# Queries of six heads by block products, and half of the sums of weight blocks on GpSimd

## The chip, the cores and the metric

The kernel runs on one core of one Trainium2 chip. The metric is the device time of one execution in microseconds (us), as the median over runs. Engines go by the profile's names: PE is TensorE's matmuls and PEld its weight loads, DVE is VectorE, ACT ScalarE, POOL GpSimd, SP SyncE (it issues the DMAs).

## The reference

A small decoder: 16 meta tokens ahead of 512 tokens, D = 1024, two layers. Each layer normalizes, projects into q, k, v and a gate z, mixes the tokens, normalizes each head's output, multiplies by silu(z) and projects back. Layer 1 is gated linear attention with 4 heads (keys of 256, values of 512), layer 2 differential attention with 8 heads of 256 columns:

```python
proj = xn @ w_in                      # layer 2: [528, 1024] x [1024, 8192]
q, k, v, z = jnp.split(proj, 4, axis=-1)
s = einsum('bhpqd,bhpkd->bhpqk', qb, kh) * scale + bias   # scale = 128 ** -0.5
p = softmax(where(dist >= 0, s, -inf))
a = p[:, :, 0] - lam * p[:, :, 1]     # two softmaxes per head
o = head_rms(einsum('bhqk,bhkv->bhqv', a, vh)) * gnorm * (1.0 - lambda_init)
y = (silu(z) * o) @ w_out
```

Nearly all of the arithmetic lies in the projections with w_in and w_out.

## The kernel before, in words

Every matrix is kept as a sum of a high and a low part in the matmul's fp32r format, and a product is made of three matmul passes (high by high, high by low, low by high). `split` (L235) makes the parts: ACT copies the high one (L240), DVE subtracts it for the low one (L241; with a scale, ACT L243 and DVE L244).

A projection of 256 output columns is made in one of two ways. The **plain** way (`project`, L340; its matmul is L347) runs, for each half of 128 columns, 24 matmuls of up to 512 tokens: 8 blocks of the inner dimension by three passes, 48 in all for the 512 real tokens. The other is a **unit** (`Unit`, L360): it takes the [1024, 256] weight block as 2 x 2 blocks of [512, 128], and the tokens as 2 x 2 blocks as well, and makes the four output blocks from seven block products in place of eight. Each product (`product`, L351; its matmul is L357) has 12 matmuls of 256 columns (real tokens, the operand set Xr) or 264 (all 528 tokens, the set X). The price is sums of blocks: of the tokens once, of the weights in every unit, of the products on the way out of PSUM (ACT's copies `u` at L378, DVE's adds L403, L405 and L407).

The weights of a unit come in `want_unit` (L285). Two DMAs bring the four blocks into a tile `raw` of [128, 4, 512] (two such tiles in the ring). From it are made, in this order, the parts a11, sums, s21, a12, s43, a22. Three of them are splits of a single block (tiles a11h and a11l, and so on). `sums` makes three adds on [128, 512] on DVE (L296): raw2 + raw3 into `sum`, that plus raw0 into `sum`, and raw2 + raw0 in place. `s21` is the split of the pair `sum` into `wh` and `wl` of [128, 1024]. `s43` first makes the fourth add, raw1 + sum0 in place, also on DVE at L296, and then splits the pair raw1, raw2. A part is made as soon as the `Weights` object finds room for it: two pairs, one sum, one each of a11, a12 and a22; the room of `sum` is given back with the fourth add.

In layer 1 the jobs q, k, v and z have 20 units; in layer 2, the z, v and k of heads 1 to 7 are 21 units, and q of all eight heads is plain. That is 41 units. `q_diff_q` (L1441) makes q of one head in layer 2 and splits it with the scale into the tiles s.q.

The order of the work is that of the program on TensorE: the class `Weaver` (L73) holds a queue of generators (the projections) and puts pieces of them between the steps of the heads' attention, so many microseconds of estimated cost at a time (`fill`); `finish` runs one to its end. Each job is queued with a cost (10.3 for a plain q, 8.9 for a unit on Xr). A unit that has a unit behind it in the queue (`following`) runs the latter's first product inside its own end. The other engines' orders are set by a scheduler from the program's order and its priorities (functions marked `urgent` come 100 ahead).

POOL has little to do. `rstd_of` (L465) makes 1/sqrt of a sum of squares: a DVE scale (L467), then a `pow` on POOL (L468). In layer 1 the rows of each head's output go through ACT's sum of squares (L1087), `rstd_of`, ACT's scaling (L1089), transposes on TensorE (L1111) and DVE's product with the gate (L1113). In layer 2, `values` does the same with a pow at L1509 between ACT's L1507 and L1510, and TensorE's transposes are L1516; scores, values and turns are L326, L1502, L1486 and L1487.

Of the kernel before, what the change touches and what calls it, by code (L numbers as in the profile page):

```python
# [12 lines left out]
F32R = mybir.dt.float32r  # L13
I32 = mybir.dt.int32
AF = mybir.ActivationFunctionType
ALU = mybir.AluOpType
# [3 lines left out]
P = 128  # L20
# [3 lines left out]
NR = 512  # L24
# [48 lines left out]
class Weaver:  # L73
# [5 lines left out]
    def add(self, gen, us=0.0):  # L79
        self.queue.append(gen)  # L80
        self.left += us
        return gen
# [102 lines left out]
def trunk(ctx, tc, x, meta, g_norm, gla_w_in, gla_w_gate_up, gla_b_gate, gla_gnorm, gla_w_out,  # L185
# [3 lines left out]
    act, dve, pe, pool, sp = nc.scalar, nc.vector, nc.tensor, nc.gpsimd, nc.sync  # L189
# [17 lines left out]
    def T(p, shape, dt, tag, **kw):  # L207
        uid[0] += 1
        return p.tile(shape, dt, tag=tag, name=f"{tag}_{uid[0]}", **kw)
# [19 lines left out]
    def urgent(fn):  # L229

        def run(*a, **kw):
            with tc.high_priority(offset=100):
                return fn(*a, **kw)
        return run
# [47 lines left out]
    def block_pair(src):  # L282
        wh, wl = w_pair([P, 2, 512])
        split(wh, wl, src)
        return [[t[:, i, :] for t in (wh, wl)] for i in range(2)]  # L285

    def want_unit(w, c0):
        def single(tag, b):
            def fn(raw):
                t = [T(wp, [P, 512], F32R, tag + part, bufs=1) for part in "hl"]  # L290
                split(*t, raw[:, b, :])
                return t
            return Part(tag, fn)

        def add(o, a, b):
            dve.tensor_tensor(o, a, b, op=ALU.add)  # L296

        def sums(raw):
            t = T(wp, [P, 2, 512], F32, "sum", bufs=1)
            add(t[:, 1, :], raw[:, 2, :], raw[:, 3, :])  # L300
            add(t[:, 0, :], t[:, 1, :], raw[:, 0, :])
            add(raw[:, 2, :], raw[:, 2, :], raw[:, 0, :])
            return t

        def outer(raw):
            add(raw[:, 1, :], raw[:, 1, :], su.t[:, 0, :])
            ws.room["sum"] += 1
            return block_pair(raw[:, 1:3, :])

        a11, a12, a22 = single("a11", 0), single("a12", 1), single("a22", 3)  # L310
        su = Part("sum", sums)
        s21 = Part("pair", lambda raw: block_pair(su.t))
        s43 = Part("pair", outer)
        ws.want((w, c0), [a11, su, s21, a12, s43, a22])
        return a11, a12, a22, s21, s43

# [1051 lines left out]
    def tok_tile():  # L1368
        return T(ep, [P, 2 * (256 + NM)], F32, "t", bufs=3)
# [68 lines left out]
                tail(i)  # L1438
        return W.add(gen(), 10.3)

    def q_diff_q(hd, s):  # L1441
        want_diff(256 * hd)

        def gen():
            for i in range(2):
                bank = pb_tile("bx" if hd else ("bv", "by")[i])
                yield from project(ws.take(), real2, None, NR, [by_halves(bank)])
                assert not hd or heads[hd - 1].scored
                if i == 0:
                    s.q = [T(ep, [P, 2, NR], F32R, f"q{j}", bufs=1) for j in range(2)]  # L1450
                urgent(split)(*[t[:, i, :] for t in s.q], bank, scale=-float(P) ** -0.5)
        return W.add(gen(), 10.3)

    def diff_steps(hd, s, ys):
# [167 lines left out]
    for hd in range(D_HEADS):  # L1622
# [9 lines left out]
        if not last:  # L1632
            n = heads[hd + 1]
            late = hd == D_HEADS - 2
            if not late:
                gates.append(q_diff_z(hd + 1, n))
                values.append(q_diff_v(hd + 1, n))
            W.stop = q_diff_k(hd + 1, n)
            projs.append(q_diff_q(hd + 1, n))
            if late:  # L1640
                values.append(q_diff_v(hd + 1, n))
                gates.append(q_diff_z(hd + 1, n))
# [94 lines left out]
```

## Time and profile before

| | |
|---|---|
| median of 3 runs | 1001.82 us (1000.56 to 1002.53) |
| the profiled execution | 1001.37 us |
| its span, from the first to the last instruction | 999.6 us (1.77 us lie around it) |
| matmuls | 7143 |
| instructions of DVE, ACT, POOL | 1586, 1304, 68 |
| HBM read | 83.64 MB |

The profile is of one execution. Busy times are sums of instruction durations; an engine's busy time can hide under another's. A row of groups reads: line, engine, operation, out<-in, shapes, count | busy us, mean ns of one | idle time ahead of them and what ended it. A row of the timeline begins with start and length in us. `PE ps L1111 <- ACT t L1089` in the waits is TensorE at L1111 that waited for ACT's tile t from L1089: total us, times, longest.

### The profile page before, as it was taken

What the parts mean: (1) busy time and instruction counts of PE and PEld (TensorE: products, weight loads), DVE (VectorE), ACT (ScalarE), POOL (GpSimd) and SP (SyncE); (2) the same over time, 40 slices, a digit from 0 to 9 for tenths busy, and PEclk for the clock granted to TensorE, in tenths of its full rate; (3) what the DMA queues carried; (4) which work ended last, traced back from release to release, by engine and by line L of the source; (5) the groups of instructions that cost most, each with busy time, mean ns of one, the idle gap of its engine ahead of it and who ended that gap; (6) DMA issues with size and microseconds to landing.
All of it is one profiled execution on the core that took longest, in us unless ns stands there. A gap on an engine that the chain in (4) does not pass through costs nothing.

```text
span 999.6 us, 18267 instructions
## 1 busy us (share of the span) xinstructions
PE 981.0 (98%) x7143; PEld 920.2 (92%) x7143; DVE 784.1 (78%) x1586; ACT 597.5 (60%) x1304; POOL 46.6 (5%) x68
## 2 busy tenths in 40 slices
PE   8999999999999999999999999999999999999997
PEld 6998999999999989999899898899998999988896
DVE  7998886777777787556998886888966879777785
ACT  7775755265535656536567666466664666645583
POOL 1000000001000100000000100000010010000001
PEclk9999999999999999999999999999999999999998
DMA  7322322141233322222231322333222332323212
GB/s 194 82 69 64 86 85 86 48 113 52 85 85 85 85 54 74 86 85 79 84 104 49 94 82 95 85 96 85 85 96 72 87 91 70 109 64 92 85 65 84
DMA packets 121161, 84.24 MB, mean 84 GB/s; under 512 B 6365, under 2 KB 110077, under 8 KB 121072
## 3 DMA queue, kind: packets, MB, share of 16 engines
q1 hardware_dynamic: 121072, 83.05, 28.8%
q8 instruction: 56, 0.92, 0.4%
q14 instruction: 33, 0.27, 0.1%
HBM read 83.64 MB, written 2.12 MB: 86 GB/s over the span
## 4 chain that ended last, share of the span: by engine, by line
PE 78%; DVE 6%; ACT 3%; DMA 3%; issue 1%; POOL 1%; SPq 0%; POOLq 0%; DVEq 0%; ACTq 0%
PE bx L357 15%; PE bx L347 10%; PE bv L357 9%; PE by L357 8%; PE ps L326 7%; PE bx L830 4%; PE bx L326 3%; PE bv L830 2%; PE by L830 2%; DMA raw<-in_gla_w_in_dram 2%; PE ps L1048 2%; PE by L326 2%; PE bv L326 2%; DVE wl L241 1%; PE by L347 1%
## 5 line engine op out<-in xcount | busy, mean ns | idle before, releaser
L240 ACT ACTIVATE wh<-raw 128x1024 fp32r<-128x1024 f32 x99 | 104.4, 1055 | 61.6 <-PE by L830 26.8
L241 DVE TENSOR_TENSOR wl<-raw,wh 128x1024 fp32r<-128x1024 f32 x99 | 121.0, 1222 | 22.0 <-ACT wh L240 14.6
L357 PE MATMUL bv<-x,wh 128*128 128x264 f32 (+1 forms) x656 | 97.5, 286 | 0.0
L357 PE MATMUL bx<-x,wh 128*128 128x264 f32 (+1 forms) x640 | 95.6, 286 | 1.2 <-ACT u L378 1.2
L357 PEld LDWEIGHTS bx<-x,wh 128*128 128x128 f32 x640 | 84.8, 188 | 2.3 <-ACT u L378 1.4
L357 PEld LDWEIGHTS bv<-x,wh 128*128 128x128 f32 x656 | 86.4, 189 | 0.3
L241 DVE TENSOR_TENSOR wl<-sum,wh 128x1024 fp32r<-128x1024 f32 x41 | 50.1, 1222 | 21.0 <-ACT wh L240 17.6
L378 ACT ACTIVATE u<-bx 128x264 f32<-128x264 f32 (+1 forms) x120 | 45.5, 380 | 33.1 <-PE bx L357 29.2
L347 PE MATMUL bx<-x,wh 128*128 128x512 f32 (+1 forms) x256 | 62.4, 385 | 0.0
L1473 ACT ACTIVATE p<-p,st 128x528 f32<-128x528 f32 (+3 forms) x64 | 36.4, 569 | 40.0 <-DVE st L1471 39.9
L357 PE MATMUL bv<-x,wl 128*128 128x264 f32 (+1 forms) x328 | 56.4, 286 | 0.0
L240 ACT ACTIVATE wh<-sum 128x1024 fp32r<-128x1024 f32 x41 | 43.2, 1055 | 19.2 <-PE by L830 9.6
L357 PE MATMUL bx<-x,wl 128*128 128x264 f32 (+1 forms) x320 | 54.5, 285 | 0.0
L347 PEld LDWEIGHTS bx<-x,wh 128*128 128x128 f32 x256 | 44.5, 188 | 7.9
L1509 POOL TENSOR_TENSOR st<-st,mhalf 128x1 f32<-128x1 f32 x32 | 26.5, 828 | 474.9 <-ACT on L1507 426.9
L357 PE MATMUL by<-x,a12h 128*128 128x264 f32 (+1 forms) x320 | 46.9, 285 | 0.0
L357 PEld LDWEIGHTS bv<-x,wl 128*128 128x128 f32 x328 | 46.2, 189 | 0.0
L357 PE MATMUL bx<-x,a11h 128*128 128x264 f32 (+1 forms) x320 | 46.2, 285 | 0.0
L357 PEld LDWEIGHTS bx<-x,wl 128*128 128x128 f32 x320 | 45.3, 188 | 0.1
L240 ACT ACTIVATE a11h<-raw 128x512 fp32r<-128x512 f32 x41 | 25.7, 628 | 32.6 <-DMA raw<-in_diff_w_in_dram 18.2
L357 PEld LDWEIGHTS bx<-x,a11h 128*128 128x128 f32 x320 | 42.2, 189 | 0.8
L357 PEld LDWEIGHTS by<-x,a12h 128*128 128x128 f32 x320 | 41.9, 188 | 0.2 <-issue 0.2
(465 smaller groups left out, 2643.4 us busy)
## 6 DMA issues: line engine op xcount, KB each, us to landing
raw<-in_gla_w_in_dram SPq DMA_DIRECT2D x48, 512.0 KB, 5.3
raw<-in_diff_w_in_dram SPq DMA_DIRECT2D x42, 512.0 KB, 4.2
raw<-in_diff_w_in_dram SPq DMA_DIRECT2D x11, 1024.0 KB, 5.7
raw<-in_gla_w_out_dram SPq DMA_DIRECT2D x8, 1024.0 KB
raw<-in_diff_w_out_dram SPq DMA_DIRECT2D x8, 1024.0 KB, 4.9
T<-bdr SPq DMA_DIRECT2D x8, 264.0 KB
out_dram<-x SPq DMA_DIRECT2D x8, 256.0 KB, 2.0
kd<-steep SPq DMA_DIRECT2D x4, 400.0 KB
```

The costliest lines, as they stand in the source:

```text
L240: act.activation(hi, src, AF.Copy)
L241: dve.tensor_tensor(lo, src, hi.bitcast(F32), op=ALU.subtract)
L326: pe.matmul(ps, l, r, start=first and n == 0, stop=last and n == 2, **kw)
L347: pe.matmul(bank, a[:, k, :], b[k] if n0 is None else b[k][:, n0 + i * nn:n0 + (i + 1) * nn], start=n == 0 and ks[0] == 0, stop=n == len(t ...
L357: pe.matmul(bank[:, :x[q].shape[2]], w[p][:, k * P:(k + 1) * P], x[q][:, k, :], start=first and i == 0, stop=i == len(PASSES) - 1, skip_gr ...
L378: act.activation(t, self.bx[:, :self.n], AF.Copy, scale=self.sc)
L830: pe.matmul(banks[i][:, :HT], h.t[p][:, k, mm * P:(mm + 1) * P], s.y[q][k][:, i * HT:(i + 1) * HT], start=n == 0, stop=n == len(PASSES) - 1)
L1048: pe.matmul(o, s.kd[:, i, kc], s.qs[:, i, t0:t0 + n], start=i == 0, stop=i == 1)
L1473: act.activation(p[:, :nk], p[:, :nk], AF.Exp, scale=-1.0, bias=st[:, m:m + 1], accum_out=st[:, 2 + m:3 + m])
L1509: pool.tensor_tensor(ms, ms, mhalf[:, :1], op=ALU.pow)
```

## The change

Two things. First, in `want_unit` the third add (raw2 + raw0) and the fourth (raw1 + sum0) go to POOL, and the fourth is issued right behind the a12 split, since that is the last that reads raw1 alone; the room of `sum` is given back there, and `s43` is only a pair's split. This holds for every unit. Second, q of heads 1 to 6 in layer 2 is made by units on the real tokens (Xr), with the scale in the adds out of PSUM and a split from a token tile `t` behind them; head 0 and head 7 keep the plain way. That makes 47 units in place of 41, and the k unit of heads 1 to 6 now has a unit behind it in the queue.

```diff
-        def add(o, a, b):
-            dve.tensor_tensor(o, a, b, op=ALU.add)
+        def add(eng, o, a, b):
+            eng.tensor_tensor(o, a, b, op=ALU.add)
 
         def sums(raw):
             t = T(wp, [P, 2, 512], F32, "sum", bufs=1)
-            add(t[:, 1, :], raw[:, 2, :], raw[:, 3, :])
-            add(t[:, 0, :], t[:, 1, :], raw[:, 0, :])
-            add(raw[:, 2, :], raw[:, 2, :], raw[:, 0, :])
+            add(dve, t[:, 1, :], raw[:, 2, :], raw[:, 3, :])
+            add(dve, t[:, 0, :], t[:, 1, :], raw[:, 0, :])
+            add(pool, raw[:, 2, :], raw[:, 2, :], raw[:, 0, :])
             return t
 
-        def outer(raw):
-            add(raw[:, 1, :], raw[:, 1, :], su.t[:, 0, :])
+        def second(raw):
+            t = a12s.fn(raw)
+            add(pool, raw[:, 1, :], raw[:, 1, :], su.t[:, 0, :])
             ws.room["sum"] += 1
-            return block_pair(raw[:, 1:3, :])
-
-        a11, a12, a22 = single("a11", 0), single("a12", 1), single("a22", 3)
-        su = Part("sum", sums)
+            return t
+
+        a11, a12s, a22 = single("a11", 0), single("a12", 1), single("a22", 3)
+        su, a12 = Part("sum", sums), Part("a12", second)
         s21 = Part("pair", lambda raw: block_pair(su.t))
-        s43 = Part("pair", outer)
+        s43 = Part("pair", lambda raw: block_pair(raw[:, 1:3, :]))
...
-    def q_diff_q(hd, s):
+    def q_diff_q(hd, s, blocks=False):
+        sc, qts = -float(P) ** -0.5, []
+
+        def parts(i):
+            assert not hd or heads[hd - 1].scored
+            if not hasattr(s, "q"):
+                s.q = [T(ep, [P, 2, NR], F32R, f"q{j}", bufs=1) for j in range(2)]
+            return [t[:, i, :] for t in s.q]
+
+        def dst():
+            qts.extend([tok_tile()[:, :NR], tok_tile()[:, :NR]])
+            return qts
+
+        @urgent
+        def tail(i):
+            split(*parts(i), qts[i])
+
+        if blocks:
+            return W.add(Unit(want_unit(d_w_in, 256 * hd), Xr, sc, dst, tail), 8.9)
...
-            projs.append(q_diff_q(hd + 1, n))
+            projs.append(q_diff_q(hd + 1, n, not late))
```

Line numbers of the changed kernel are one higher from there on (L468 becomes L469, L357 L358), and 16 higher behind `q_diff_q` (L1516 becomes L1532, L1502 L1518, L1486 L1502).

The order on **POOL** in head 1 of layer 1 (`st` are the sums of squares of the head's five blocks of rows, `raw` the weight blocks, numbers tell tiles apart). Before:

```order
L468 TENSOR_TENSOR st_5548<-st_5548,mhalf 16x1
L468 TENSOR_TENSOR st_5620<-st_5620,mhalf 128x1
L468 TENSOR_TENSOR st_5683<-st_5683,mhalf 128x1
L468 TENSOR_TENSOR st_5773<-st_5773,mhalf 128x1
L468 TENSOR_TENSOR st_5850<-st_5850,mhalf 128x1
```

And now, at the same place:

```order
L296 TENSOR_TENSOR raw_5390<-raw_5390 128x512
L469 TENSOR_TENSOR st_5548<-st_5548,mhalf 16x1
L296 TENSOR_TENSOR raw_5390<-raw_5390,sum_5530 128x512
L469 TENSOR_TENSOR st_5621<-st_5621,mhalf 128x1
L296 TENSOR_TENSOR raw_5574<-raw_5574 128x512
L469 TENSOR_TENSOR st_5684<-st_5684,mhalf 128x1
L469 TENSOR_TENSOR st_5773<-st_5773,mhalf 128x1
L296 TENSOR_TENSOR raw_5574<-raw_5574,sum_5720 128x512
L296 TENSOR_TENSOR raw_5713<-raw_5713 128x512
L469 TENSOR_TENSOR st_5851<-st_5851,mhalf 128x1
L296 TENSOR_TENSOR raw_5713<-raw_5713,sum_5906 128x512
```

Third adds (raw alone) and fourth adds (raw with sum) now stand between the five pows.

**DVE** at the same place, around the scale (L467) that releases the second pow. Before:

```order
L1113 TENSOR_TENSOR t_5610<-ps_5605,z_5282 128x4x16
L241 TENSOR_TENSOR wl_5593<-sum_5530,wh_5592 128x1024
L241 TENSOR_TENSOR y_1038_5604<-t_5610,y_1037_5603 128x4x16
L241 TENSOR_TENSOR a12l_5597<-raw_5390,a12h_5596 128x512
L467 TENSOR_SCALAR st_5620<-st_5620 128x1
L296 TENSOR_TENSOR raw_5390<-raw_5390,sum_5530 128x512
```

And now:

```order
L241 TENSOR_TENSOR a12l_5597<-raw_5390,a12h_5596 128x512
L1114 TENSOR_TENSOR t_5611<-ps_5606,z_5282 128x4x16
L241 TENSOR_TENSOR wl_5593<-sum_5530,wh_5592 128x1024
L241 TENSOR_TENSOR y_1038_5605<-t_5611,y_1037_5604 128x4x16
L468 TENSOR_SCALAR st_5621<-st_5621 128x1
L296 TENSOR_TENSOR sum_5720<-raw_5574 128x512
```

The a12 split has moved ahead of the split of the sums, the fourth add is gone, and the first sum of the next unit has come up behind the scale.

**PE** in layer 2, where q of head 2 is made between the steps of head 1 (`bx`, `bv` and `by` are banks of PSUM that take the products, `on` the normalized rows of head 1). Before:

```order
L347 MATMUL bx_10383<-x_1531_8630,wh_10287 128x512
L347 MATMUL bx_10383<-x_1528_8627,wl_10288 128x512 x4
L347 MATMUL bx_10383<-x_1530_8629,wl_10288 128x512
L1516 MATMUL ps_10430<-ident,on_10395 128x128 x2
L347 MATMUL bx_10383<-x_1530_8629,wl_10288 128x512 x3
L326 MATMUL ps_10440<-v_1641_9345,aT_1847_10417 128x256
L326 MATMUL ps_10440<-v_1642_9346,aT_1847_10417 128x256
L326 MATMUL ps_10440<-v_1641_9345,aT_1848_10418 128x256
L1502 MATMUL ps_10440<-vm_9347,am_10416 128x256
```

And now:

```order
L358 MATMUL bx_10419<-x_1557_8855,wh_10382 128x256 x5
L358 MATMUL bx_10419<-x_1557_8855,wl_10383 128x256 x4
L1532 MATMUL ps_10521<-ident,on_10453 128x128 x2
L358 MATMUL bv_10530<-x_1556_8854,wh_10382 128x256 x6
L327 MATMUL ps_10537<-v_1641_9346,aT_1869_10505 128x256
L327 MATMUL ps_10537<-v_1642_9347,aT_1869_10505 128x256
L327 MATMUL ps_10537<-v_1641_9346,aT_1870_10506 128x256
L1518 MATMUL ps_10537<-vm_9348,am_10504 128x256
L358 MATMUL bv_10530<-x_1556_8854,wh_10382 128x256 x2
L358 MATMUL bv_10530<-x_1556_8854,wl_10383 128x256 x4
```

The steps of head 1 stand between matmuls of 256 columns of a unit in place of 512 columns of the plain form.

More of the change, by code (lines that the diff above doesn't have):

```diff
@@ L1447, in gen @@
                 yield from project(ws.take(), real2, None, NR, [by_halves(bank)])
[L1448 to L1451, printed above, removed]
+                urgent(split)(*parts(i), bank, scale=sc)
         return W.add(gen(), 10.3)
```

## The prediction

> **What bounds the kernel now.** I read the busy times first, then the waits of TensorE, then the chain that ended last, and only then the groups of DVE and POOL. The page's first part, for the profiled execution:
>
> ```profile
> span 999.6 us, 18267 instructions
> PE 981.0 (98%) x7143; PEld 920.2 (92%) x7143; DVE 784.1 (78%) x1586; ACT 597.5 (60%) x1304; POOL 46.6 (5%) x68
> PEclk9999999999999999999999999999999999999998
> ```
>
> TensorE is busy for 98% of the span at full clock; POOL does 68 small things. What TensorE waits for (us in total, times, longest):
>
> ```profile
> PE ps L734 <- DVE t L403: 1.5, 1, 1.5
> PE bx L357 <- ACT u L378: 1.2, 1, 1.2
> PE ps L1111 <- ACT t L1089: 0.7, 2, 0.4
> ```
>
> These are the three of the thirteen waits that lie at places the change touches, and none is for a weight tile of a unit. So the kernel is bound by its matmuls, and what saves matmul time saves time, as long as the engines that feed them keep up. Whether they have room differs by stage. Columns: stretch, sum, then busy us of PE, PEld, DVE, ACT, POOL, the granted clock, DMA share and rate:
>
> ```profile
> 500.00:520.00 20.00, 20.00 (x142) 18.77 (x141) 19.72 (x32) 13.06 (x25) 0.00 (x0) 1.00 0.27 73
> 520.00:540.00 20.00, 20.00 (x166) 19.99 (x166) 19.64 (x54) 14.64 (x34) 0.00 (x0) 1.00 0.29 77
> 653.00:703.00 50.00, 50.00 (x375) 47.68 (x374) 40.22 (x79) 32.84 (x76) 3.82 (x4) 1.00 0.32 91
> ```
>
> In the 40 us where the diff layer begins, DVE is at 98 to 99% and TensorE still has no gap; elsewhere DVE has a fifth free (40.22 of 50).
>
> **Part 1: q of six heads as units (TensorE).** The chain of waits, q of head 2 in the old form (L347, 512 columns, 48 matmuls), then two of the block products that other heads' units run on the same real tokens (L357, 256 columns, 12 matmuls each). Columns: start, length, what.
>
> ```profile
> 740.94 2.78 PE bx L347 x12
> ...
> 743.94 1.40 PE bx L347 x6
> ...
> 745.56 0.70 PE bx L347 x3
> ...
> 746.73 3.51 PE bx L347 x15
> ...
> 750.46 2.79 PE bx L347 x12
> ...
> 779.43 1.41 PE bx L357 x12
> ...
> 783.79 1.42 PE bx L357 x12
> ```
>
> Old: 2.78 + 1.40 + 0.70 + 3.51 + 2.79 = 11.18 us. New: seven products of 1.415 = 9.9 us. Saved: 1.28 us a head, **7.7 us for six heads**. These pieces lie end to end on the chain, so nothing covers them and all of it is span.
>
> **Part 2: what a unit more costs DVE and ACT, and what leaves DVE.** From the groups (count | busy, mean ns):
>
> ```profile
> L296 DVE TENSOR_TENSOR raw<-raw,sum 128x512 f32<-128x512 f32 x41 | 28.2, 688 | 0.6
> L296 DVE TENSOR_TENSOR raw<-raw 128x512 f32<-128x512 f32 x41 | 28.1, 685 | 0.1
> L241 DVE TENSOR_TENSOR a11l<-raw,a11h 128x512 fp32r<-128x512 f32 x41 | 28.2, 687 | 9.5 <-ACT a11h L240 9.4
> L403 DVE SCALAR_TENSOR_TENSOR t<-bv,u 128x264 f32<-128x264 f32 x26 | 11.1, 427 | 6.9 <-ACT u L378 6.6
> L244 DVE SCALAR_TENSOR_TENSOR q<-bx,q 128x512 fp32r<-128x512 f32 x14 | 9.6, 685 | 0.1
> ```
>
> The first two rows are the adds that go to POOL: 41 x (0.688 + 0.685) = 56 us leave DVE. A q unit has the same two pair splits as plain q, and adds three single splits (3 x 0.687), two sums (2 x 0.687), four adds out of the banks (4 x 0.427) and a split of two halves in place of two old ones of 0.685, which cancel: 5.1 us, 31 us for six. DVE ends near 760 us of busy time, some 25 less than before. TensorE's path pays nothing for this, since DVE has idle time where q runs, and 19.72 of 20 is eased by two adds a unit. The cover is DVE's free fifth; without it each q unit would cost its 5.1 us, 31 in all.
>
> q itself comes later after its last matmul: an add (0.43) and a split where there was a split alone. Before scores follows W.fill(3.0) or second-layer matmuls, 3 us of covering work against 0.5 us more. I take nothing; without that cover it is 0.5 x 6 = 3 us.
>
> **Part 3: 94 adds on POOL.** The trace has no POOL add of this size. The nearest rows:
>
> ```profile
> L1509 POOL TENSOR_TENSOR st<-st,mhalf 128x1 f32<-128x1 f32 x32 | 26.5, 828 | 474.9 <-ACT on L1507 426.9 <-DVE wl L241 33.5 <-issue 7.3
> ...
> L468 POOL TENSOR_TENSOR st<-st,mhalf 16x1 f32<-16x1 f32 x4 | 2.2, 541 | 315.0 <-DVE st L467 315.0
> ...
> L645 POOL COPY y<-t 128x64 f32<-128x64 f32 x2 | 0.5, 238 | 2.8 <-PE ps L588 1.5 <-PE by L588 1.3
> ...
> L1716 POOL MEMSET const-float32-1.0<- 128x1 f32 x1 | 0.1, 99 | 0.0
> ```
>
> Low end: DVE's own 0.69 us. High end: the copy takes (238 - 99) / 63 = 2.2 ns a column more than the one-column memset, so 512 columns from one input take 1.2 us, and doubled for two inputs 2.3. I take 1.2, the copy's slope being the nearest row; the two ends give 94 x 0.69 = 65 and 94 x 2.3 = 216 us of POOL's time, in a span where it has 950 free. Throughput is no issue; who waits is. The Trainium skill (GPSIMD Engine Reference, section 3.1 Elementwise) gives 4497 ns for an add of 2048 fp32 columns; a quarter of it, as an estimate, is 1.12 us, which would leave the sum as it is.
>
> The third add feeds the s43 pair with the fourth. In the tight stage the split of a pair ends this long before its use:
>
> ```profile
> 535.56 1.22 DVE L241 TENSOR_TENSOR wl<-raw,wh 128x1024 fp32r<-128x1024 f32 x1
> ...
> 540.10 0.65 PE L357 MATMUL bx<-x,wl 128*128 128x264 f32 x4
> ```
>
> That is 540.10 - 536.78 = 3.3 us, the least that I found there for a pair. An add slower by 0.5 to 1.6 us, and issued one part earlier than before, eats at most half of it: nothing lost.
>
> What stands behind the adds in POOL's queue is the rstd of the heads' norms (L468, L1509), and here there are places without slack. GLA head 1, its second block of rows:
>
> ```profile
> 225.33 0.69 DVE L241 TENSOR_TENSOR a12l<-raw,a12h 128x512 fp32r<-128x512 f32 x1
> 225.94 0.15 DVE L467 TENSOR_SCALAR st<-st 128x1 f32<-128x1 f32 x1
> 226.05 0.69 DVE L296 TENSOR_TENSOR raw<-raw,sum 128x512 f32<-128x512 f32 x1
> 226.16 0.99 POOL L468 TENSOR_TENSOR st<-st,mhalf 128x1 f32<-128x1 f32 x1 [4.43 <-DVE st L467]
> 227.19 0.69 ACT L1089 ACTIVATE t<-ps,st 128x512 f32<-128x512 f32 x1 [1.62 <-POOL st L468]
> 227.94 0.66 PE L1111 MATMUL ps<-ident,t 128*128 128x128 f32 x4
> ```
>
> DVE's scale at 225.94 releases POOL's pow, that releases ACT's at 227.19, and TensorE's transposes start 0.06 us after ACT ends. In the order of the changed kernel the fourth add (raw_5390 with sum_5530) stands ahead of this pow on POOL, and DVE's a12 split, which it waits for, has moved ahead of wl<-sum: so the add can begin with wl<-sum, 1.22 + 0.22 + 0.15 = 1.6 us before the pow is released. Left alone it is done in time, and the pow, with no DVE add beside it, takes 0.54 in place of 0.99: 0.45 gained. Held back by wl<-sum (both inputs in SBUF; the rival on sharing shows that case) it begins 0.4 us before the pow's release and makes it late by 1.2 - 0.4 - 0.45, some 0.4, and with the next sum of DVE beside it by 0.7; an add of 2.3 us that starts only with the release gives 2.3 - 0.45 = 1.85. I take 0.7, since of the two cases the rows show the held one. Head 2 has the same constellation (pow at 332.30). **Lost: 1.4 us**, by the ends -0.9 to 3.7. Where the order puts a third add ahead of a pow, that add's input has been in for longer, and I take it as done.
>
> In the diff layer the rows have more room, mostly 1.7 to 5.5 us. One of the few that has not:
>
> ```profile
> 749.13 0.47 ACT L1510 ACTIVATE on<-ps,st 128x256 f32<-128x256 f32 x1 [1.07 <-POOL st L1509]
> ...
> 750.08 0.38 PE L1516 MATMUL ps<-ident,on 128*128 128x128 f32 x2
> ```
>
> 0.48 us of slack. I count about eight such rows of 32, of which an add stands in front of perhaps two: 2 x (1.2 - 0.5) = 1.4; I take **1 us**, since such an add must also come in the last microsecond before the pow. Against this, DVE's relief may take some of the waits of units away: I take 0.2 us.
>
> **Sum**, against the profiled execution's own 1001.37 us: -7.7 + 1.4 + 1.0 - 0.2 = -5.5, so 995.9. The median shown is 0.45 above that execution, so **996.3 us** in the median of runs. By the ends of the unknown terms: -7.7 - 0.9 - 0.2 = -8.8 (993.0), and with q uncovered and adds of 2.3 us -7.7 + 3.7 + 2 + 3 = +1.0 (1002.8).
>
> **The rivals.** *Half is lost to the sharing of POOL and DVE.* What the two do to each other is in these rows:
>
> ```profile
> 539.52 1.22 DVE L241 TENSOR_TENSOR wl<-sum,wh 128x1024 fp32r<-128x1024 f32 x1
> 540.14 1.60 POOL L1509 TENSOR_TENSOR st<-st,mhalf 128x1 f32<-128x1 f32 x1 [65.03 <-ACT on L1507]
> 540.65 0.68 DVE L296 TENSOR_TENSOR raw<-raw,sum 128x512 f32<-128x512 f32 x1
> ```
>
> A pow of 0.54 took 1.60 and ended 0.41 after the second of two DVE instructions with two SBUF inputs; DVE's kept their length. So POOL yields, and in a stage where DVE issues such instructions back to back, a POOL add could be held for several microseconds. Then s43 is late by more than the lead of 3.3 where leads are least. Two to five such delays of 0.7 us in the units, beside the 2.4 above, lose 1.4 to 3.5 us more: 998 to 1000. For it: the row. Against it: most leads are twice as long, and fewer DVE adds leave more gaps.
>
> *Slower: the lock falls on DVE.* A POOL add is much longer than a pow, and if it begins first, DVE's next instruction with two SBUF inputs may wait for all of it. In 500 to 540, where DVE is 98 to 99% busy, three units pass, six adds: 6 x (1.2 to 2.3) = 7 to 14 us of blocked DVE for 6 x 0.69 = 4.1 us taken off it, net 3 to 10 us, which TensorE pays once the lead of 3.3 is gone; the rest of the chain pays through late rstd in the ten zero-slack rows of GLA heads 1 and 2, at one add each up to 10 x 1.2 = 12 us. It ends slower when these two sum to over 7.7 us: from about 0.8 us on each of the ten rows, or adds over 2 us in the dense stage. With half of the rows' 12 and the whole of the dense stage it is 9 to 16 less 7.7, +1.3 to +8.3: 1003 to 1010. No row shows DVE held by POOL, but none has a POOL instruction that could. The Trainium skill (SBUF — State Buffer, section Who interferes with whom) says that DVE and GpSimd share a port pair, that a DVE instruction with two SBUF inputs contends with one of GpSimd that reads SBUF, and that whoever issues first has the pair for the whole instruction while the other fully blocks. The trace agrees for the blocked POOL (1.60 against 0.54); by that rule DVE would be blocked as often, and this rival would be the result.
>
> *Nothing comes of it:* the units are made as the diff says (the order shows 84 matmuls of 256 columns for q), so only a loss equal to the gain gives 1000 to 1003.8.
>
> **How the numbers follow.** Forecast 58% (993 to 998), a somewhat larger gain 3%, half lost 12%, nothing 9%, slower 18%. No change means within 0.2%, 2 us, about what a measurement of this kernel can tell apart: three quarters of the half-lost case is faster than 999.8. Faster 0.58 + 0.03 + 0.09 = 0.70, same 0.03 + 0.09 = 0.12, slower 0.18. The range goes from 992.5, below the forecast's good end, to 1005, into the slower case: about 0.12 of it and the rest of the larger gain, 0.02, stay outside. The likeliest sign's own range is 993 to 999.8.
>
> **What would show it.** Right: six heads' q in 256-column products of 1.41 us; POOL adds near 1.2 us; DVE near 760 us busy; TensorE's idle time up by 2 to 3 us, at L1112 behind L1090, and nowhere at a weight tile. Wrong: POOL adds over 2 us or stretched by DVE; TensorE waits at L358 on wh or wl of a unit; DVE instructions longer than their lengths above; a new wait at the scores for q. The prediction fails first on the price of the POOL add and on who yields to whom.

## The result and the profile after

The changed kernel takes **1036.96 us** (median of 6 runs, 1034.3 to 1039.26) against 1001.96 us before (6 runs, 1000.56 to 1002.85): a ratio of 1.035, 95% interval 1.0333 to 1.0367. It is 35 us slower, where 5.5 us faster was forecast, and lies 32 us above the top of the range. The profiled execution (1039.26 us) has this on the page:

```profile
span 1037.5 us, 18880 instructions
PE 992.6 (96%) x7359; PEld 935.5 (90%) x7359; DVE 813.9 (78%) x1558; ACT 610.6 (59%) x1340; POOL 183.7 (18%) x162
PEclk8999999999999999999999999999999999999999
```

Three things differ from what was forecast. DVE has 28 instructions fewer, and was to end near 760 us of busy time; it has 813.9. TensorE has 216 matmuls more, as it should, but its idle time went from 18.6 us (999.6 - 981.0) to 44.9. And the granted clock is no longer full everywhere. Where DVE's time went, by its groups (count | busy us, mean ns | idle before):

```profile
L241 DVE TENSOR_TENSOR wl<-raw,wh 128x1024 fp32r<-128x1024 f32 x93 | 121.8, 1310 | 17.9 <-ACT wh L240 16.3 <-PE bx L348 1.0
L241 DVE TENSOR_TENSOR wl<-sum,wh 128x1024 fp32r<-128x1024 f32 x47 | 66.6, 1418 | 32.2 <-ACT wh L240 28.8 <-PE bx L348 1.7 <-PE bv L358 1.4
L296 DVE TENSOR_TENSOR sum<-sum,raw 128x512 f32<-128x512 f32 x47 | 47.1, 1001 | 0.3
L241 DVE TENSOR_TENSOR a11l<-raw,a11h 128x512 fp32r<-128x512 f32 x47 | 39.0, 831 | 10.2 <-ACT a11h L240 9.8
```

The same groups before (the fourth, a11l with 687 ns, stands in the prediction):

```profile
L241 DVE TENSOR_TENSOR wl<-raw,wh 128x1024 fp32r<-128x1024 f32 x99 | 121.0, 1222 | 22.0 <-ACT wh L240 14.6 <-PE bx L347 6.7 <-PE by L347 0.2
L241 DVE TENSOR_TENSOR wl<-sum,wh 128x1024 fp32r<-128x1024 f32 x41 | 50.1, 1222 | 21.0 <-ACT wh L240 17.6 <-PE bv L357 1.5 <-PE bx L347 1.3
L296 DVE TENSOR_TENSOR sum<-sum,raw 128x512 f32<-128x512 f32 x41 | 28.1, 685 | 0.2
```

So 1310, 1418, 1001 and 831 ns stand against 1222, 1222, 685 and 687. Summed over DVE's instructions, what is longer than the median of the same form before, by over 60 ns, makes 56 us in some 70 instructions beside a busy POOL, and under 1 us in all others. That is about what 814 is above 760. POOL's adds:

```profile
L296 POOL TENSOR_TENSOR raw<-raw 128x512 f32<-128x512 f32 x47 | 72.5, 1542 | 339.4 <-DVE sum L296 320.3 <-ACT wh L240 10.3 <-DVE st L1493 8.8
L296 POOL TENSOR_TENSOR raw<-raw,sum 128x512 f32<-128x512 f32 x47 | 66.6, 1418 | 213.8 <-DVE a12l L241 155.3 <-ACT u L379 19.9 <-DVE t L233 16.8
```

The shortest of each take 1.28 us, near the 1.2 of the prediction; the means are 0.14 to 0.26 longer, since POOL waits for DVE as well. TensorE's waits, the longest sums:

```profile
PE bx L358 <- ACT u L379: 3.6, 5, 1.3
PE ps L1112 <- ACT t L1090: 3.4, 6, 0.7
PE bv L358 <- DVE t L406: 3.3, 3, 1.5
PE bv L358 <- DVE t L404: 3.0, 3, 1.4
PE ps L735 <- DVE t L404: 2.5, 1, 2.5
```

None is on a weight tile. TensorE stands at banks of PSUM that DVE or ACT has not yet emptied (bv, bx), and at small results of the same two engines. One such wait from its start, in the timeline of layer 1:

```profile
225.43 0.69 DVE L296 TENSOR_TENSOR sum<-sum,raw 128x512 f32<-128x512 f32 x1
225.48 1.79 POOL L296 TENSOR_TENSOR raw<-raw 128x512 f32<-128x512 f32 x1 [1.99 <-DVE sum L296]
226.04 1.78 DVE L241 TENSOR_TENSOR a11l<-raw,a11h 128x512 fp32r<-128x512 f32 x1
227.74 0.42 DVE L404 SCALAR_TENSOR_TENSOR t<-by,u 128x264 f32<-128x264 f32 x1
228.21 1.25 PE L358 MATMUL by<-x,a12h 128*128 128x264 f32 x8 [0.71 <-DVE t L404]
```

DVE's first sum releases its own second sum (225.43) and POOL's third (225.48) in the same moment. DVE is first, so POOL stands for half a microsecond and takes 1.79 in place of 1.28. Then POOL has its turn, and now DVE's a11l (0.69 alone), begun at 226.04, takes 1.78, since POOL is not done until 227.27. Behind it in DVE's order is the add that empties bank by, and TensorE waits 0.71 us for that bank. Both engines give way, to whoever was first. Over the whole trace, 79 of the 94 adds overlap a DVE instruction with both inputs in SBUF: in 43 of them POOL had begun first, and in 42 of these a DVE instruction is longer than its median before; in 36 DVE had begun first, and 35 of these adds are longer than 1.34 us.

The longest waits have a second price. The longest of the list, in the timeline, has the same pattern (am has 32 x 16 elements):

```profile
382.50 1.77 POOL L296 TENSOR_TENSOR raw<-raw 128x512 f32<-128x512 f32 x1 [3.23 <-DVE sum L296]
383.18 1.12 DVE L337 TENSOR_TENSOR am<-t,am 32x16 fp32r<-32x16 f32 x1
384.33 0.43 DVE L404 SCALAR_TENSOR_TENSOR t<-by,u 128x264 f32<-128x264 f32 x1
...
384.82 0.40 PE L735 MATMUL ps<-ident,t 128*32 128x128 f32 x1 [2.52 <-DVE t L404]
```

And the windows of 5 us (columns as in the prediction: sum, then PE, PEld, DVE, ACT, POOL, the granted clock, DMA):

```profile
20.00:25.00 5.00, 4.94 (x21) 4.64 (x22) 5.00 (x8) 2.66 (x5) 0.00 (x0) 0.50 0.36 14
80.00:85.00 5.00, 4.58 (x24) 4.37 (x25) 3.42 (x6) 2.65 (x3) 0.68 (x1) 0.66 0.03 8
385.00:390.00 5.00, 5.00 (x22) 4.16 (x22) 4.04 (x9) 2.24 (x6) 0.00 (x0) 0.50 0.20 57
```

Besides the last microseconds, where the kernel before has it too, the clock was at a half in three places, for 6.8, 3.4 and 6.8 us by its records, which costs half of 17, 8.5 us. The third begins at the end of that wait. The first lies ahead of the first POOL add (65.8 us), where both kernels do the same: it is not in the profile before, but q_only's, with no POOL add, has 3.4 us of half clock at the same place. So not all of the 8.5 is the change's. Over the six runs the mean granted clock was 0.990 to 0.996, and 0.995 to 0.997 in the runs of the kernel before beside q_only; as an estimate from these means (0.993 against 0.996, of 1037 and 1002 us), some 3 of the 35 us are half clock, and the two runs at 0.996 still took 1034.3 and 1036.3 us. The second and third follow matmuls whose starts are 2.1 and 2.8 us apart; one pair 2.0 us apart, at 147, has no half clock behind it, and pool_only (below) has one 2.75 us apart, at 383, without. So the length of one pause does not decide it. The Trainium skill (TensorE: Matmul & The Clock Gate, Part 1) gives an idle window of about 3.4 us as what brings the half clock; here it was recorded behind shorter pauses.

### The profile page after: what moved, and what is told of

The parts are those of the page before. It is cut to its first block, busy times and chain, and to the rows that moved or that the text cites. A ratio compares the mean times of both kernels' runs of the same rounds, so it can differ in the third digit from the quotient of the medians.

```text
span 1037.5 us, 18880 instructions
## 1 busy us (share of the span) xinstructions
PE 992.6 (96%) x7359; PEld 935.5 (90%) x7359; DVE 813.9 (78%) x1558; ACT 610.6 (59%) x1340; POOL 183.7 (18%) x162
## 4 chain that ended last, share of the span: by engine, by line
PE 52%; DVE 18%; ACT 8%; DMA 5%; issue 5%; POOL 3%; SPq 0%; POOLq 0%; DVEq 0%; ACTq 0%
PE bx L358 10%; PE bv L358 5%; PE by L358 5%; PE bx L831 4%; DVE wl L241 4%; PE ps L327 4%; PE bx L348 3%; DVE sum L296 3%; PE bx L327 3%; PE bv L831 2%; PE by L831 2%; DMA raw<-in_gla_w_in_dram 2%; PE ps L1049 2%; DMA raw<-in_diff_w_in_dram 2%; ACT wh L240 2%
## 5 line engine op out<-in xcount | busy, mean ns | idle before, releaser
L241 DVE TENSOR_TENSOR wl<-raw,wh 128x1024 fp32r<-128x1024 f32 x93 | 121.8, 1310 | 17.9 <-ACT wh L240 16.3
L296 POOL TENSOR_TENSOR raw<-raw 128x512 f32<-128x512 f32 x47 | 72.5, 1542 | 339.4 <-DVE sum L296 320.3
L358 PE MATMUL bv<-x,wh 128*128 128x264 f32 (+1 forms) x752 | 112.2, 287 | 8.1 <-DVE t L406 3.3
L358 PE MATMUL bx<-x,wh 128*128 128x264 f32 (+1 forms) x736 | 113.7, 289 | 3.8 <-ACT u L379 3.6
L358 PEld LDWEIGHTS bv<-x,wh 128*128 128x128 f32 x752 | 98.9, 189 | 10.0 <-DVE t L406 4.0
L358 PEld LDWEIGHTS bx<-x,wh 128*128 128x128 f32 x736 | 98.5, 189 | 7.0 <-ACT u L379 5.7
L296 POOL TENSOR_TENSOR raw<-raw,sum 128x512 f32<-128x512 f32 x47 | 66.6, 1418 | 213.8 <-DVE a12l L241 155.3
L241 DVE TENSOR_TENSOR wl<-sum,wh 128x1024 fp32r<-128x1024 f32 x47 | 66.6, 1418 | 32.2 <-ACT wh L240 28.8
L379 ACT ACTIVATE u<-bx 128x264 f32<-128x264 f32 (+1 forms) x138 | 52.4, 380 | 37.8 <-PE bx L358 34.8
L358 PE MATMUL bx<-x,wl 128*128 128x264 f32 (+1 forms) x368 | 62.5, 286 | 0.0
L358 PE MATMUL bv<-x,wl 128*128 128x264 f32 (+1 forms) x376 | 61.8, 284 | 0.0
L358 PE MATMUL by<-x,a12h 128*128 128x264 f32 (+1 forms) x368 | 55.0, 288 | 1.5 <-DVE t L404 1.4
L358 PE MATMUL bx<-x,a11h 128*128 128x264 f32 (+1 forms) x368 | 53.9, 285 | 0.0
L358 PEld LDWEIGHTS bx<-x,wl 128*128 128x128 f32 x368 | 52.0, 190 | 0.1
L358 PEld LDWEIGHTS bv<-x,wl 128*128 128x128 f32 x376 | 52.0, 188 | 0.0
L358 PEld LDWEIGHTS by<-x,a12h 128*128 128x128 f32 x368 | 48.7, 191 | 2.6 <-DVE t L404 2.1
L358 PEld LDWEIGHTS bx<-x,a11h 128*128 128x128 f32 x368 | 48.4, 189 | 0.5
```

The lines of the kernel that those rows point to most:

```text
L241: dve.tensor_tensor(lo, src, hi.bitcast(F32), op=ALU.subtract)
L296: eng.tensor_tensor(o, a, b, op=ALU.add)
L358: pe.matmul(bank[:, :x[q].shape[2]], w[p][:, k * P:(k + 1) * P], x[q][:, k, :], start=first and i == 0, stop=i == len(PASSES) - 1, skip_gr ...
L379: act.activation(t, self.bx[:, :self.n], AF.Copy, scale=self.sc)
```

## The experiments

Theory, called the lock: an add on POOL that reads SBUF and a DVE instruction with two inputs in SBUF exclude each other, and DVE's order passes each delay on to TensorE. Rivals: the six q units, and the queue (rstd behind adds in POOL's order, s43's split waiting for POOL). Ratios are to the kernel before on the same chip, with 95% intervals.

**q_only.** The change's `want_unit` is put back, its q units stay.

```diff
-            add(pool, raw[:, 2, :], raw[:, 2, :], raw[:, 0, :])
+            add(raw[:, 2, :], raw[:, 2, :], raw[:, 0, :])
...
-            add(pool, raw[:, 1, :], raw[:, 1, :], su.t[:, 0, :])   # behind the a12 split
+            add(raw[:, 1, :], raw[:, 1, :], su.t[:, 0, :])         # in s43, as before
```

> The six q units of the change, with all four sums of every unit on DVE as before. Lock theory (a POOL add that reads SBUF holds back DVE's instructions with two SBUF inputs for as long as it runs): without POOL adds the matmul saving of 7.7 us is kept but for 1 to 4 us of new waits, since DVE takes 6 x 6.5 = 39 us more: 994 to 999 us, no DVE group longer than before, no stretch at half clock beyond the last. Rival (the units' extra work on DVE and ACT is what delays TensorE): 1010 us or more.

1004.63 us, ratio 1.0014 (1.0005 to 1.0024): no loss to speak of, and no gain either. The rival that blames the units for the 35 us falls; the forecast's term for them falls too (below).

**pool_only.** The reverse: `want_unit` of the change in the kernel before, q plain.

> The 41 units of before with the third and fourth add on POOL, q plain. Lock theory: 82 adds hold DVE for some 45 us, and the loss of the change comes with them: 1025 to 1045 us, DVE's sums and low parts longer as in the changed kernel. Rival (the q units): 1000 to 1005 us.

1019.9 us, ratio 1.0164 (1.0147 to 1.0181). Less than expected, but with the sign and the marks of the theory: 47.5 us of DVE's time stretched beside POOL. In its trace DVE takes the first scores of layer 2 18.0 us later than before (540.2 against 522.2 us), and behind that only 1.5 us are lost.

**idle_add and idle_memset.** The kernel before with all its DVE adds, and beside them POOL work that nobody needs.

```diff
+        def idle(src):                       # idle_add
+            pool.tensor_tensor(scr, src[:, :448], src[:, :448], op=ALU.add)
...
+        def idle(src):                       # idle_memset
+            pool.tensor_copy(scr[:, :1], src[:, :1])
+            for _ in range(3):
+                pool.memset(scr, 0.0)
...
+            idle(t[:, 0, :])                 # behind the third add
+            idle(t[1].bitcast(F32))          # behind the a12 split
```

> The kernel before, all four sums still on DVE, with two POOL adds more per unit (128x448, both inputs from SBUF, result into a scratch tile that nothing reads), issued where the change issues its adds; nothing of the computation waits for them but the release of the tile that they read. Lock theory: 1020 to 1050 us, as bad as pool_only or worse, since DVE keeps its adds. Queue theory (the rstd that stand behind the adds in POOL's order are late, and s43's splits wait for POOL): no s43 waits for POOL here, so 1002 to 1015 us, the same as idle_memset.

> As idle_add, but in place of each add a copy of one column (so that it starts at the same moment) and three memsets of 128x448 of the scratch tile, which read nothing from SBUF. POOL is busy at the same places for about as long, and the rstd stand behind it in the same order. Lock theory: DVE's groups keep their lengths, 1001 to 1009 us. Queue theory: the same time as idle_add.

idle_add: 1025.1 us, 1.022 (1.0203 to 1.0237). idle_memset: 1006.65 us, 1.0041 (1.0027 to 1.0055). This is the pair that settles it. The same places in POOL's order; a group of a copy and three memsets even keeps POOL busy longer (0.38 or 0.57 + 3 x 0.48 us) than an add (1.1 to 1.4):

```profile
L311 POOL MEMSET scr<- 128x448 bf16 x246 | 117.1, 476 | 14.0
...
L309 POOL CAST scr<-a12l 128x1 bf16<-128x1 f32 x41 | 23.3, 567 | 124.9 <-DVE a12l L241 98.9 <-DVE t L233 14.2 <-DVE st L481 8.8
L309 POOL CAST scr<-sum 128x1 bf16<-128x1 f32 x41 | 15.6, 380 | 362.6 <-DVE sum L298 302.8 <-DVE st L1491 35.0 <-DVE st L1490 24.8
```

DVE beside the memsets, and then DVE beside the adds (two of its groups in each kernel):

```profile
L241 DVE TENSOR_TENSOR wl<-sum,wh 128x1024 fp32r<-128x1024 f32 x41 | 50.1, 1221 | 19.9 <-ACT wh L240 15.5 <-PE bv L371 1.5 <-PE bx L361 1.3
...
L298 DVE TENSOR_TENSOR raw<-raw 128x512 f32<-128x512 f32 x41 | 28.0, 684 | 0.1
```

```profile
L241 DVE TENSOR_TENSOR wl<-sum,wh 128x1024 fp32r<-128x1024 f32 x41 | 58.1, 1418 | 15.6 <-ACT wh L240 12.8 <-PE bx L359 1.3 <-PE bv L369 1.1
...
L298 DVE TENSOR_TENSOR raw<-raw 128x512 f32<-128x512 f32 x41 | 33.4, 814 | 0.1
```

1221 and 684 ns beside memsets, within a nanosecond of the kernel before; 1418 and 814 beside adds. The stretch is 1.7 us in all against 38.6. The idle add also holds its input tile for longer than the one-column copy does, but DVE's recorded waits for POOL are the same, 6.5 us in idle_add and 6.4 in idle_memset. So it is not that POOL is busy, nor what waits behind it: it is that POOL reads SBUF. What the queue does by itself is the 4 us of idle_memset.

**pool_gla and pool_diff.** The change, with POOL's adds in one layer only (`here = w is not d_w_in`, or `is`, chooses).

> The change with its q units, but POOL makes the two adds only in the 20 units of layer 1; layer 2's units keep them on DVE with the fourth in s43. If the loss of the adds lies in layer 1 whatever comes behind it (pool_only reached the first scores of layer 2 18 us late and lost 1.5 behind them): q_only's 1.5 us plus 17, 1018 to 1024 us. Rival (the loss of the change lies where q units and POOL's adds meet): 1003 to 1010 us.

> The counterpart: q units, POOL adds only in the 27 units of layer 2. In the changed kernel the stretch from the first scores to the end takes 18 us longer than in pool_only, though each part alone costs 1.5 us there. Lock and q units together (DVE at 81% with the units, held by POOL on top): 1016 to 1024 us. If the two only add up: 1004 to 1007 us.

1018.34 us (1.0147, 1.0121 to 1.0173) and 1024.82 us (1.022, 1.0195 to 1.0245). Over q_only the adds cost 13 us in layer 1 and 21 in layer 2, together the 34 that the change loses over q_only. Counted in the profiled executions from the first scores of layer 2 to the end, they cost 1.5 us with plain q (pool_only) and 17 with the units (496.7 us in pool_diff against q_only's 479.6). That would fit if plain q, 11 us of matmuls that need two pair splits, had been the time in which DVE made up for being held; idle_add_q below tries it.

**nopow_after and nopow_before.** The heads' pow leaves POOL's queue; the inverse root of their norms is left out.

```diff
-            pool.tensor_tensor(ms, ms, mhalf[:, :1], op=ALU.pow)
+            dve.tensor_scalar(ms, ms, 0.0, 1.0, op0=ALU.mult, op1=ALU.add)
```

(and the same for the rows of layer 1.)

> The changed kernel, with the heads' pow taken off POOL: a DVE instruction of one column writes 1.0 in its place (the inverse root of the heads' norms is left out), so that nothing of the heads waits behind an add in POOL's queue. Queue theory: most of the loss goes, 1000 to 1012 us. Lock theory: the adds still hold DVE, 1024 to 1036 us, less only by what nopow_before gains as well and some 3 to 6 us of rstd behind adds.

> The same in the kernel before: what the way through POOL costs without any adds (the inverse root of the heads' norms is left out). Ten rows of heads 1 and 2 in layer 1 without slack, 0.4 to 0.8 us each: 995 to 1000 us under either theory; it is the reference for nopow_after.

1025.78 us (1.0223, 1.0204 to 1.0243) and 999.22 us (0.9965, 0.9953 to 0.9976). Between the two lie 26.6 us; with the pows in place it is 35. So the queue is a smaller part, at most some 8 us, and the rest of 27 stays with none of the heads' pows behind the adds. Some 2 of the 8 are likely half clock (mean 0.993 in the six runs of the changed kernel, 0.995 in nopow_after), which this pair does not keep apart. What that part looks like in the changed kernel, in layer 2:

```profile
694.73 1.29 POOL L296 TENSOR_TENSOR raw<-raw,sum 128x512 f32<-128x512 f32 x1 [7.89 <-DVE t L233]
...
695.98 0.55 POOL L1525 TENSOR_TENSOR st<-st,mhalf 128x1 f32<-128x1 f32 x1
...
696.56 0.48 ACT L1526 ACTIVATE on<-ps,st 128x256 f32<-128x256 f32 x1 [2.49 <-POOL st L1525]
696.93 1.05 ACT L240 ACTIVATE wh<-sum 128x1024 fp32r<-128x1024 f32 x1
...
698.01 1.23 DVE L241 TENSOR_TENSOR wl<-sum,wh 128x1024 fp32r<-128x1024 f32 x1 [3.28 <-ACT wh L240]
699.15 0.42 DVE L404 SCALAR_TENSOR_TENSOR t<-bv,u 128x264 f32<-128x264 f32 x1
...
699.63 0.75 PE L358 MATMUL bv<-x,wh 128*128 128x264 f32 x4 [1.37 <-DVE t L404]
```

The pow waits for the add, ACT stands 2.49 us at the pow's result with a weight split queued behind it, DVE stands 3.28 us at that split with the add for bank bv queued behind, and TensorE stands at the bank for 1.37 us. One microsecond in POOL's order goes through three other orders.

**early_dve, third_pool, fourth_pool.** The change with both adds on DVE at their new places, with the third alone on POOL, with the fourth alone.

```diff
-            add(pool, raw[:, 1, :], raw[:, 1, :], su.t[:, 0, :])
+            add(dve, raw[:, 1, :], raw[:, 1, :], su.t[:, 0, :])     # early_dve, third_pool
...
-            add(pool, raw[:, 2, :], raw[:, 2, :], raw[:, 0, :])
+            add(dve, raw[:, 2, :], raw[:, 2, :], raw[:, 0, :])      # early_dve, fourth_pool
```

> The change with all four sums on DVE, the fourth still as soon as a12 is split: the new place in DVE's order (next unit's first sum comes up, the sum tile is given back earlier) without POOL. Lock theory: as q_only, 1001 to 1008 us. Rival (the order is the cause: DVE stands at sums that wait for their DMA, and late parts): 1012 us or more.

> The change with only the third add on POOL (47 adds, not 94), the fourth early on DVE. Lock theory: half of POOL's busy time on adds, half of the 33 us that POOL's adds cost beyond q_only: 1015 to 1025 us. If it is the fourth add alone (it stands between the heads' rstd and is s43's last input): 1001 to 1008 us.

> The counterpart, only the fourth add on POOL, the third on DVE. Lock theory: 1015 to 1025 us. If it is the third alone: 1001 to 1008 us.

1004.87 us (1.0024, 1.0014 to 1.0034), 1031.63 us (1.0297, 1.0279 to 1.0314), 1015.02 us (1.0126, 1.0108 to 1.0143). The new order costs nothing. The two adds are far from equal: the third, beyond both ranges of its expectation, does most of the harm. It is released by DVE's first sum while DVE's second is queued, and each of the 47 holds up a DVE instruction, in 22 of them that second sum; of the fourth adds 15 meet no DVE instruction with both inputs in SBUF. The stretch is 40.4 us against 21.4 for the fourth, whose largest part (7.9) is at wl<-sum. Half of third_pool's stretch is the second sum's:

```profile
L296 DVE TENSOR_TENSOR sum<-sum,raw 128x512 f32<-128x512 f32 x47 | 51.7, 1100 | 0.3
```

(third_pool; 682 ns in fourth_pool.)

**idle_add_q.** q_only with idle_add's POOL work.

> q_only with the two idle POOL adds of idle_add in all 47 units: lock on top of the q units, no s43 that waits for POOL, no add taken off DVE. If the lock alone explains why the two parts cost 17 us more together in layer 2 than apart: 1032 to 1048 us, with the stretches between the first scores of the heads as long as in the changed kernel (55.9, 54.2, 79.6, 53.3, 80.0 us). If s43's wait for POOL is needed for that: 1020 to 1028 us.

1033.38 us (1.0306, 1.0289 to 1.0323). Nearly the loss of the whole change comes with adds whose results nobody reads; s43 waits for nothing here, and the heads' periods (from DVE's first scores of one to those of the next: 56.2, 54.7, 78.2, 54.4, 78.2 us) are near those of the changed kernel (55.8, 54.2, 79.7, 53.3, 80.0). From the first scores of layer 2 to the end, the idle adds cost 7.4 us with plain q (idle_add's 484.8 us against 477.4) and 12.4 with the units (492.0 against q_only's 479.6): the units do take away something that hid the lock, though that is 5 us of the some 15 by which the change there exceeds the sum of its parts (18.3 us, against 1.5 in pool_only and 2.2 in q_only). The rest was not taken apart.

**q_light and q_1to4.** Why do the q units give nothing by themselves? q_light leaves 7 of DVE's instructions out of each q unit; q_1to4 gives units to heads 1 to 4 only, on early_dve.

```diff
+                if light:                    # q_light, in q's units
+                    t = T(wp, [P, 512], F32R, tag + "h", bufs=1)
+                    act.activation(t, raw[:, b, :], AF.Copy)
+                    return [t, t]
...
-            projs.append(q_diff_q(hd + 1, n, not late))
+            projs.append(q_diff_q(hd + 1, n, hd < 4))      # q_1to4
```

> q_only, with DVE's share of the six q units cut by 7 instructions of 128x512 each (4.8 of some 6.5 us a unit): their four sums and the low parts of a11, a12 and a22 are left out (raw blocks and high parts stand in, so q of these heads is not the reference's). TensorE's 84 matmuls a head stay as they are. If DVE's load is what ate the units' saving: 6 us less than q_only or more, 996 to 999 us. If ACT's or PSUM's share does it, or the saving on TensorE is not there at all: within 2 us of q_only, 1003 to 1006 us.

> early_dve with q units for heads 1 to 4 alone, since its trace loses 1.8 us behind head 5's scores and gains 0.9 ahead of them: 1000 to 1003 us, at best 1 us below the kernel before. It is the only version left that might beat both kernels. If a head's saving is eaten wherever the unit stands: as the kernel before, 1002 to 1004 us.

1002.98 us (1.0004, 0.9995 to 1.0013) and 1005.86 us (1.0033, 1.0021 to 1.0046). 29 us of DVE work less bring 1 us against q_only: the amount of DVE's work is not what eats the saving. Fewer units do not help either, against both ranges of the expectation.

**q_tail, early_tail, before_tail.** In q_light TensorE stood up to 0.8 us (1.0 in two waits) at the first product of q in bank bv; a unit's first split was moved behind its last add out of that bank.

```diff
                 add(1, 0, bz, self.u3, -1)
-                self.tail(1)
...
                 add(0, 1, self.bv, self.u2, 1)
+                self.tail(1)
                 self.tail(0)
```

> q_only, with the split of a unit's first finished half moved behind the unit's last add out of bank bv (both halves are split at the end). In q_light TensorE stood up to 1.0 us at the first product of q that takes bank bv, because k's split (ACT and DVE, 0.8 us) stands on DVE ahead of the add that frees it. If this seam is what ate the units' saving: 2 to 4 us less than q_only, 1000 to 1002.5 us. If the waits only move to the splits and what hangs on them: 1003 to 1006 us.

> The same edit on early_dve (q units, all sums on DVE, the fourth early). As q_tail within 1.5 us; it is the version that would beat both kernels if the seam matters: 1000 to 1003 us.

> The same edit on the kernel before, where no q unit stands behind k: the reference for the two. Seams z to v and v to k are there already and cost nothing in its trace: within 1.5 us of the kernel before, 1001 to 1004 us.

1007.24 us (1.0054, 1.004 to 1.0068), 1006.93 us (1.0045, 1.003 to 1.006), 1014.96 us (1.0127, 1.0111 to 1.0142). All slower than their references, and all above the ranges expected; the edit alone costs 12 us, since v comes late (TensorE stands 6.4 us at L326 for DVE's vm, in 4 waits). What it says of the seam is unclear, and the theory of the seam finds no support. Giving bv a second bank would have been the cleaner test; it was not tried.

**q_short.** The kernel before, with 6 of plain q's 48 matmuls left out in six heads, and nothing else.

```diff
+        todo = todo[:len(todo) - drop]
...
-                yield from project(ws.take(), real2, None, NR, [by_halves(bank)])
+                yield from project(ws.take(), real2, None, NR, [by_halves(bank)], drop=3 if 0 < hd < D_HEADS - 1 else 0)
```

> The kernel before with plain q, of which heads 1 to 6 leave out 6 of their 48 matmuls (the low part of the weights for three of the eight inner blocks): 6 x 0.232 = 1.39 us a head less on TensorE, 8.4 us in all, about what a q unit saves, and nothing else changes: splits, loads, banks and DVE's work stay. If TensorE's work bounds layer 2, as the prediction took it: 993 to 996 us. If something else sets a head's period just as well, so that a saving on TensorE alone comes back as waits: 1000 to 1003 us.

1001.0 us, ratio 0.9976 (0.9966 to 0.9986): 2.4 us for 8.4 us of matmuls. Its trace has a wait at the top of TensorE's list that the kernel before does not have:

```profile
PE ps L1517 <- ACT on L1511: 4.6, 4, 2.2
```

Those are the transposes of layer 2's normalized rows, at the end of the way through ACT, POOL's pow and ACT again. From DVE's first scores of one head to those of the next, the periods are 53.3, 53.9, 74.8, 53.7, 74.8, 53.7 us before and 53.0, 52.4, 74.0, 54.6, 73.5, 56.3 here: where no wait appears, a period loses 0.8 to 1.5 us (52.4, 74.0, 73.5), where one does, it loses little or gets longer (53.0, 54.6, 56.3; the last also has 3.4 us at half clock behind the longest of these waits).

## Why the prediction was wrong

1. *"These pieces lie end to end on the chain, so nothing covers them and all of it is span."* **This step failed.** The saving in matmul time is there: from the first scores of head 0 to those of head 6, q_only's matmuls, each taken at the median step of its shape before, need 356.1 us against 363.7, 7.6 us less as forecast. None of it becomes time (364.8 us against 364.2 for this stretch). The kernel before has no wait of TensorE over 0.15 us there; q_only has several, on engines that empty banks or bring small results, among them

```profile
PE ps L736 <- DVE vm L338: 1.4, 3, 0.6
PE ps L326 <- DVE q L241: 0.6, 1, 0.6
PE ps L1531 <- ACT on L1525: 0.5, 1, 0.5
```

In all, 13 matmuls of q_only start over 0.15 us later than that step allows, by 6.0 us together, and steps late by 0.06 to 0.15 us sum to 6.6 against 5.4. So the saving in the filler, the projections between a head's steps, came back as waits for those steps. q_short shows the same with nothing but matmuls taken away (2.4 of 8.4 us arrive). The wait for q at the scores (0.6 us; 0.7 in two waits in the changed kernel) is one that the prediction took at nothing.
2. *"TensorE's path pays nothing for this, since DVE has idle time where q runs"* (the units' 5.1 us of DVE work a head): right as to the amount of work, as q_light shows within 1 us, for as long as DVE is not held. When each result comes is another matter: most of the waits under 1 are on DVE.
3. *"DVE ends near 760 us"*: 813.9. The adds left, but what was left on DVE grew by 56 us beside POOL; q_only, with all 94 adds on DVE, has 812.6 us. And pool_only, where only the adds' engine and place change, has 782.4 us with 82 instructions fewer, against 784.1 before. Taking the adds off DVE relieved it of next to nothing.
4. *The POOL add at 1.2 us*: right (1.28 alone).
5. *"So POOL yields"*, read from a pow that was passed over by DVE: **here lies the 35 us.** The row showed the half of the rule in which DVE is first. Pows show no other half: in the trace before, no DVE instruction beside POOL is over 60 ns longer than the median of its form. Beside an add of 1.28 us DVE does meet it. The sum therefore had no term for DVE held by POOL; the runs show 56 us of it on DVE and, by idle_add against idle_memset, 18 us of time from 82 such adds alone. The prediction had the rule (the Trainium skill, SBUF — State Buffer, Who interferes with whom: whoever issues first has the port pair, the other fully blocks), and as a rival with 18%; the trace now agrees with it in both directions, and with its statement that a POOL instruction that only writes does not contend (1.7 us of stretch under 246 memsets).
6. *The price of that rival, 1003 to 1010*: too low. It held DVE back in the dense 40 us alone, and counted late rstd beside it. The traces show stretch over the whole kernel, 22.9 us in layer 1 and 33.4 in layer 2, and DVE's order passes each on.
7. *"1.4 us" for two rows behind adds*: the queue cost at most some 8 us, part of it clock (nopow pair), at six waits of L1112 (3.4 us), and through ACT's order at weights and banks, which the term did not follow.
8. *"Where the order puts a third add ahead of a pow, ... I take it as done"* and *nothing lost* at the lead of 3.3 us: right, in that TensorE never stood at a unit's weight tile (ACT's split of s43 waited for POOL twice, 1.7 us); its waits came at banks of PSUM and small results instead.

Settled: the lock is the cause of most of the loss (idle_add against idle_memset, idle_add_q), the queue of at most some 8 us. Not settled is why the q units' saving comes back whole: it goes to several waits, none of them half of it; DVE's instruction count and the choice of heads are excluded, a fixed way through ACT and POOL is shown for q_short only. No version here with the reference's computation beats the kernel before.

## What to carry to other kernels

An idle GpSimd is no free adder beside a busy VectorE: what it reads from SBUF is taken out of VectorE's time, here 0.6 us for each of 94 adds (56 / 94), about what each had cost there (0.69), and at moments that nobody chose. Before moving an operation, look in the trace for both orders of the two engines, not for one; and ask what stands behind the held instruction in its engine's order, since that, not the operation moved, is what the bound engine waits for. And where a bound engine's work is filler between steps of a chain, a saving in the filler is worth something only where the step behind it is ready earlier.

## What the runs showed of the hardware

- POOL and DVE exclude each other per instruction, both ways: an a11l of 0.69 us took 1.78 beside an add, an add of 1.28 took up to 2.67. Memsets, which only write, left DVE's groups within a nanosecond of what they were.
- In the kernel without POOL adds, taking the heads' pow off POOL gave 3.7 us (nopow_before), the inverse root left out.
- Pauses of TensorE of 2.1 and 2.8 us between starts were followed by a half clock for 3.4 and 6.8 us in the changed kernel, one of 2.0 us there and one of 2.75 us in pool_only were not.
